# A rotary query turned by 32x32 blocks on VectorE, and stored in 128-byte runs, in an encoder layer on one core

## The chip, the core and the metric

One core of a Trainium2 chip runs the kernel. Its engines work side by side, each through its own list of instructions in order: TensorE (PE in the profile, its weight loads PEld), VectorE (DVE), ScalarE (ACT), GpSimd (POOL), and SyncE (SP), which here does nothing but issue DMAs. All DMAs of SP go through one queue: SP issues them one after the other, and one that waits for a semaphore holds up those behind it. The transfers themselves run on 16 DMA engines. The metric is the device time of one execution, in microseconds (us), the median of several.

## What is computed

One encoder layer on 2048 rows of 1024 columns, float32. A projection of the input feeds two groups of four heads. Group A is a gated linear attention in two directions, computed in chunks. Group B is a latent attention: queries and keys come from a compressed row by RMSNorm and a second matrix, and 64 of the query's 192 columns are rotary.

```python
q = (rms_norm(c_q, q_norm_g) @ w_uq).reshape(B, S, MLA_HEADS, MLA_D_NOPE + MLA_D_ROPE)
q_nope = q[..., :MLA_D_NOPE] * scale
q_rope = apply_rope(q[..., MLA_D_NOPE:], positions) * scale
...
s = (jnp.einsum('bqhd,bkhd->bhqk', qn, k_nope) + jnp.einsum('bqhr,bkr->bhqk', qr, k_r))
p = jax.nn.softmax(s, axis=-1)
return jnp.einsum('bhqk,bkhv->bqhv', p.astype(v.dtype), v)
```

Both groups' outputs go through one output projection, a residual and a LayerNorm. The change touches `q_rope`, 4 heads of 64 columns, on its way from the rows of a chunk (rows in the partitions) to the layout that the attention's matmuls need (the 64 rotary columns in the partitions, rows along the free dimension).

## The kernel before

Every float32 product is made of three matmuls: each operand is split into a high part (`hi`, line 353, on ACT by default) and a low part (`lo`, line 359, a subtraction on DVE, or on POOL where "pool" is given), and `mm3` (lines 407 to 409) multiplies high by high, high by low and low by high.

The work has four stages. The *first sweep* (to about 370 us) goes over the 16 chunks of 128 rows from the last to the first: group A's projections, the parts inside a chunk and the states of one direction, stored to DRAM. The *second sweep* (`sweep_c`, about 370 to 590 us) goes over the chunks forward, in eight steps of two chunks. The *attention* (about 590 to 1110 us) goes over 16 blocks (4 groups of 512 queries by 4 heads); for each it fetches the queries from DRAM. The *output projection* ends the kernel.

What the second sweep does for a chunk, by the names in the profile: `ipm` (line 1288) projects the chunk; `rm` is the RMSNorm's factor, `cq` and `ckv` (1311, 1315, ACT) the normed rows; `tm` (1341, PE) transposes them; `cqT`, `ckvT` and `krs` are their splits. `pqr` multiplies by the rotary columns, `qrf` (1478, DVE and, for the last add, 1376, POOL) applies the rotation, giving 128 rows by 4 heads by 64. Then, before the change:

- `c_tq` (1381): PE transposes two heads at a time, 128x128, into a PSUM tile `tq` of the pool `tr` (two buffers, shared with `tm` and `pqr`).
- `c_qrTh` and `c_qrTl`: ACT copies it as the high part and DVE subtracts for the low part, both of 128x256 from PSUM, into the tiles `qrTh` and `qrTl`, one buffer each for both chunks of a step.
- `c_sqr` (1265): four DMAs of SP per step, two for each part, each of 128 partitions by 1 KB, into the DRAM tiles `rh_s` and `rl_s` of the block group.

For group A, `Ob` (1435, PE) multiplies the query by the state, with the loads `qdb`, `SU`, `oib` and `ub` (1396, SP) from DRAM; `oib` is added on DVE (1438), then `og` (1458, DVE) norms and gates the result; a PSUM buffer of the pool `gp` comes free after it, which the next `Ob`, `pz` or `pq` needs. `oT` (1464) turns `og` by VectorE's 32x32 transposes, and `c_soT` (1470) stores it in four DMAs whose access patterns put the blocks in their places, in 128-byte runs, 64 KB each. Per step, `pz` (1217) projects the gate of group B from both chunks, `gm` is its SiLU, stored by `gm_s` (1238), and `pq` makes the other 128 query columns of each head, split into `qah` and `qal`, stored by `c_sqa` (1259).

**What sets the order.** Each function of the second sweep has a place: tables `PLACE_C`, `PLACE_C_FIRST` (step 0) and `PLACE_C_LAST` (step 7) give a pair of numbers for the two chunks, or one number for the step. `sweep_c` adds the step's number, sorts all by that sum and records them in this order with `in_order`, which makes each engine, SP too, keep it. So in SP's list the stores of step 5's rotary queries (5 + 1.869 = 6.869) stand right before the load of `oib` for chunk 14 (7 - 0.124 = 6.876), and those of step 6 (7.869) before chunk 14's `oa_s` (8.09). On ACT, chunk 14's `qrTh` (7 + 1.065) stands before chunk 15's `ckv` (7 + 1.075).

The attention has its own `in_order` list. Its first members on SP are the fetches of blocks 0 and 1 (lines 1520 and 1524: `qh`, `ql`, `rh`, `rl`, each `r` tile by two DMAs, one for each copy of the 64 rows, since the keys' high and low parts lie one under the other). They need buffers of the pool `wz`, which hold the weights of `pz` till the last `pz` of step 7. The two SP lists are merged when the kernel is built; neither is reordered in itself. Tiles with `bufs=1` are rewritten only when all that read them, DMAs too, have finished.

Of the kernel before, what the change touches and what calls it, by code (L numbers as in the profile page):

```python
# [9 lines left out]
F32 = mybir.dt.float32  # L10
F32R = mybir.dt.float32r
# [7 lines left out]
P = 128  # L19
# [4 lines left out]
H = 4  # L24
# [5 lines left out]
QB = 512  # L30
NQB = S // QB
# [113 lines left out]
    Ob=(0.141, 0.861),  # L145
    tm=(0.532, 1.152),
    pqr=(0.849, 1.355),
    tq=(1.06, 1.482),
    xh=(-0.19, -0.054),
    sqO=(0.272, 0.988),  # L150
    rgl=(0.283, 1.029),
# [6 lines left out]
    cqTh=(0.624, 1.184),  # L158
    ckvTh=(0.64, 1.277),
    krT=(0.848, 1.233),  # L160
    qrTh=(1.16, 1.587),
    oT=(0.392, 1.103),
    oib=(0.24, 0.881),
    ss=(0.278, 1.005),
# [5 lines left out]
    cqTl=(0.758, 1.284),  # L170
    ckvTl=(0.687, 1.321),
    qrf=(0.853, 1.411),
    qrTl=(1.25, 1.687),
    xl=(-0.154, 0.109),
    M=(-0.337, 0.299),
    Sf1=(-0.582, 0.202),
# [42 lines left out]
    Ob=(0.066, 0.896),  # L219
    tm=(0.445, 1.143),  # L220
    pqr=(0.716, 1.336),
    tq=(1.11, 1.512),
    xh=(-0.3, 1.403),
    sqO=(0.469, 0.999),
    rgl=(0.603, 1.027),
# [9 lines left out]
    qrTh=(1.276, 1.598),  # L235
# [11 lines left out]
    qrTl=(1.322, 1.703),  # L247
# [31 lines left out]
    Ob=(0.0, 0.299),  # L279
    tm=(0.495, 1.083),  # L280
    pqr=(0.749, 1.284),
    tq=(0.919, 2.161),
    xh=(-0.262, -0.109),
    sqO=(0.15, 0.374),
    rgl=(0.229, 0.457),
# [9 lines left out]
    qrTh=(1.065, 2.174),  # L295
# [11 lines left out]
    qrTl=(1.081, 2.186),  # L307
# [35 lines left out]
class K:  # L343
# [145 lines left out]
    def run(self):  # L489
        tc, nc, ins = self.tc, self.nc, self.ins  # L490
        with ExitStack() as top:
            cp = top.enter_context(tc.tile_pool(name="const", bufs=1))
            self.cp = cp
            dp = top.enter_context(tc.tile_pool(name="scr", bufs=1, space=DRAM))
            self.qd_s = [dp.tile([P, H * P], F32, name=f"qd_s{c}") for c in range(NCH)]
            self.oi_s = [dp.tile([P, H * P], F32, name=f"oi_s{c}") for c in range(NCH)]
            self.su_s = [dp.tile([P, H * P], F32, name=f"su_s{c}") for c in range(NCH)]
            self.u_s = [dp.tile([P, H * P], F32, name=f"u_s{c}") for c in range(NCH)]
            self.qa_s = [[dp.tile([P, H, QB], F32, name=f"q{p}_s{b}") for p in "hl"] for b in range(NQB)]
            self.qr_s = [[dp.tile([H, 64, QB], F32, name=f"r{p}_s{b}") for p in "hl"] for b in range(NQB)]  # L500
            self.gm_s = [dp.tile([P, H, QB], F32, name=f"gm_s{b}") for b in range(NQB)]
            self.oa_s = [dp.tile([P, H, P], F32, name=f"oa_s{c}") for c in range(NCH)]
            self.qk_s = [[dp.tile([64, H, P], F32, name=f"{n}_s{c}") for c in range(NCH)] for n in ("qx", "kx")]
            self.r_s = [dp.tile([1, H, QB], F32, name=f"r_s{b}") for b in range(NQB)]
            self.ob_s = [dp.tile([P, H, QB], F32, name=f"ob_s{b}") for b in range(NQB)]

            ident = cp.tile([P, P], F32, name="ident")
            self.ident = ident
            self.gkv_c = cp.tile([P, 1], F32, name="gkv_c")
            self.gn_c = cp.tile([P, 1], F32, name="gn_c")  # L510
            self.cw = cp.tile([P, NCH, 3, H], F32, name="cw")

            psum = ExitStack()
            pspool = lambda n: psum.enter_context(tc.tile_pool(name=n, bufs=2, space=PSUM, reuse_waits="tile"))
            self.gp, self.ip, self.tr = pspool("gp"), pspool("ip"), pspool("tr")
            self.xfp = top.enter_context(tc.tile_pool(name="xfp", bufs=2, reuse_waits="tile"))
            edge = top.enter_context(tc.tile_pool(name="edge", bufs=1, side="right"))
            edge.tile([P, 8], F32, name="edge")
            self.keep = top.enter_context(tc.tile_pool(name="keep", bufs=1, side="right", reuse_waits="tile"))
            wgs = ExitStack()  # L520
            self.wgp = wgs.enter_context(tc.tile_pool(name="wgp", bufs=2 * NK + 1, side="right", reuse_waits="tile"))
            self.xab = wgs.enter_context(tc.tile_pool(name="xab", bufs=2, side="right"))
            self.wgate = []
            self.wl = None
            self.sweep_a()
            self.wz = top.enter_context(tc.tile_pool(name="wz", bufs=2 * NK + 1, reuse_waits="tile"))
            bcs = ExitStack()
            self.wm = bcs.enter_context(tc.tile_pool(name="wm", bufs=2 * NK + 1, reuse_waits="tile"))
            self.bc = bcs.enter_context(tc.tile_pool(name="bc", bufs=1, reuse_waits="tile"))
            self.wl = bcs.enter_context(tc.tile_pool(name="wl", bufs=2, reuse_waits="tile"))  # L530
            self.late_gates()
            wgs.close()
            rp = top.enter_context(tc.tile_pool(name="res", bufs=1, side="right", reuse_waits="tile"))
            self.ckvT_h = rp.tile([P, NKT, P], F32R, name="ckvT_h")
            self.ckvT_l = rp.tile([P, NKT, P], F32R, name="ckvT_l")
            self.kr = rp.tile([P, NKT, P], F32R, name="krs")
            self.vh = rp.tile([P, NKT, P], F32R, name="vh")
            self.vl = rp.tile([P, NKT, P], F32R, name="vl")
            self.sweep_c()
            bcs.close()  # L540
            psum.close()
            self.wof = top.enter_context(tc.tile_pool(name="wof", bufs=PRE_W, side="right", reuse_waits="tile"))
            self.attention()
# [63 lines left out]
    def sweep_a(self):  # L607
        tc, nc, ins, cp = self.tc, self.nc, self.ins, self.cp
        with ExitStack() as ctx:
# [98 lines left out]
            step(0, {(1, 5): [("lrT", "cur")]})  # L708
            ch[1]["x"] = self.split_x(xp, xnext, NCH - 2, "xa", "dve", 2)
            run("bst", 0)  # L710
            self.wgr = [self.wgp.tile([P, 512], F32, tag="wg", name=f"wgr{k}") for k in range(NK)]
            for k, raw in enumerate(self.wgr):
# [12 lines left out]
            for i in range(4, NCH):  # L725
# [13 lines left out]
                if i == 12:  # L739
                    assert next(rope, None) is None  # L740
                    self.rope_tables(hpi)
            i = NCH - 1
            run("q", i)
            run("k", i)
            run("av", i - 1)
# [436 lines left out]
        self.wa[ct] = pa  # L1182

    def scale_w(self, ct):
        wa = self.w1.tile([P, H, P], F32, tag=f"qrT{'hl'[ct]}", name=f"wabs{ct}")
        self.nc.vector.scalar_tensor_tensor(wa, self.wa[ct], self.gq[:, ct:ct + 1],
                                            self.gkv_b[:, None, :].to_broadcast([P, H, P]), ALU.mult, ALU.mult)
        self.wa[ct] = wa
# [71 lines left out]

    def c_sqr(self, s):
        b, qs = self.of_step(s)
        for t, dst in zip(s["qrT"], self.qr_s[b]):
            for pr in range(2):
                self.nc.sync.dma_start(dst[2 * pr:2 * pr + 2, :, qs].rearrange("h d t -> (h d) t"),
                                       t[:, pr].rearrange("p a t -> p (a t)").bitcast(F32))


    def c_lx(self, d):
# [106 lines left out]
        self.nc.gpsimd.tensor_tensor(d["qr"], d["qr"], d["qrt"], ALU.add)  # L1376

    def c_tq(self, d):
        tq = d["tq"] = self.tr.tile([P, 4, P], F32, tag="tr", name=f"tq{d['c']}")
        for pr in range(2):  # L1380
            self.nc.tensor.transpose(tq[:, pr], d["qr"][:, 2 * pr:2 * pr + 2].rearrange("p h d -> p (h d)"), self.ident)

    def c_qrTh(self, d):
        s = d["step"]
        if "qrT" not in s:
            s["qrT"] = [self.w1.tile([P, 2, 2, P], F32R, tag=f"qrT{p}", name=f"qrT{p}{d['st']}") for p in "hl"]
        self.hi(s["qrT"][0][:, :, d["j"]], d["tq"][:, 0:2])

    def c_qrTl(self, d):
        qrT, j = d["step"]["qrT"], d["j"]  # L1390
        self.lo(qrT[1][:, :, j], d["tq"][:, 0:2], qrT[0][:, :, j])


    def gl_load(self, d, tag, src):
# [104 lines left out]
    def attention(self):  # L1499
        tc, nc = self.tc, self.nc  # L1500
# [3 lines left out]
        with ExitStack() as ctx:  # L1504
# [10 lines left out]
            def fetch(i):  # L1515
                h, b = blocks[i]
                q = stt[i]["q"] = []
                for p, src in zip("hl", self.qa_s[b]):
                    q.append(qp.tile([P, QB], F32R, tag="wz", name=f"q{p}{i}"))
                    nc.sync.dma_start(q[-1].bitcast(F32), src[:, h])  # L1520
                for p, src in zip("hl", self.qr_s[b]):
                    q.append(qp.tile([P, QB], F32R, tag="wz", name=f"r{p}{i}"))
                    for r in (slice(0, 64), slice(64, 128)):
                        nc.sync.dma_start(q[-1][r].bitcast(F32), src[h])

            def scores(i, j):

# [159 lines left out]
            def yc(i):  # L1687
# [3 lines left out]
                nc.sync.dma_start(self.ob_s[b][:, h], t)  # L1691

            fetch(0)
            fetch(1)
            wv = bp.tile([P, H * P], F32, tag="ofl", name="wvf", bufs=1)
            nc.sync.dma_start(wv, self.ins["wv"])
# [20 lines left out]
            for i in range(nb):  # L1717
                for j in range(NP):
                    t = NP * i + j
# [310 lines left out]
```

## Time and profile before

| | |
|---|---|
| time, 3 runs | 1277.12 us median (1277.0 to 1278.61) |
| the profiled execution | 1277.05 us; its span, first to last instruction, 1275.3 us |
| granted TensorE clock | 0.998 |
| busy in the span: PE, DVE, ACT, POOL | 1251.5, 898.4, 732.4, 720.1 us |
| PE busy from 0 to 370, 370 to 590, 590 to 1110 us | 360.88, 217.03, 517.12 us |
| DMA engines' mean share from 370 to 590 us | 0.67 |

How to read the profile's lines. A timeline row has the start in us, the duration in us, the engine, the line of the kernel, the operation, output and inputs by the program's names, shapes and the count of merged instructions; behind it in brackets stands the idle time of the engine before it and who ended it. SPq is SP's queue, and its duration is that of issuing the DMA, not of the transfer. A tile view gives for each line the count, then the shortest, median and longest duration in ns, and below "DMA to landing", from issue to arrival, in us. A row of the chain of waits has the start, how long the chain stays there, the engine, the tile and the line. A window row has the busy time of each engine in that stretch.

### The profile page before, as it was taken

Reading aid. Unit: us, or ns where it says so; the run is one execution under the profiler, and the core shown is the slowest. Engines: PE = TensorE matmul, PEld = TensorE weight load, DVE = VectorE, ACT = ScalarE, POOL = GpSimd, SP = SyncE. Lnnn points to the kernel's source line nnn. Section 1 sums busy time; section 2 is a strip of 40 time slices with the busy share of each in tenths; the row PEclk is TensorE's granted clock in tenths of the full one; section 3 lists DMA queues with packets and bytes.
Section 4 is the critical chain, followed back from the end, with each engine's and each line's share of the span. In section 5 each row is a group of like instructions: output and inputs, shape, how many; then the busy total and the mean of one; then the engine's idle time right before and its main releaser. Section 6 shows DMA issues by size and latency. Waiting matters only on the chain.

```text
span 1275.3 us, 19650 instructions
## 1 busy us (share of the span) xinstructions
PE 1251.5 (98%) x6986; PEld 1103.4 (87%) x6986; DVE 898.4 (70%) x1601; ACT 732.4 (57%) x1186; POOL 720.1 (56%) x443
## 2 busy tenths in 40 slices
PE   8999999999999999999999999999999999999997
PEld 7999999999899999989788888888888888887886
DVE  6635454544565555554888888888888888479997
ACT  7544444454565544544888888788888888511110
POOL 0132323232345555520598888889999999935541
PEclk9999999999999999999999999999999999999999
DMA  8223434334757777657201111111233110376652
GB/s 292 79 81 110 114 110 115 109 100 114 244 199 205 221 208 206 186 153 219 76 9 49 42 52 52 44 31 58 58 92 91 42 43 10 124 235 195 211 192 99
DMA packets 167233, 155.24 MB, mean 122 GB/s; under 512 B 77046, under 2 KB 119678, under 8 KB 167136
## 3 DMA queue, kind: packets, MB, share of 16 engines
q1 hardware_dynamic: 159072, 151.86, 40.0%
q0 software_dynamic: 672, 2.10, 0.4%
q8 instruction: 55, 0.90, 0.3%
q10 hardware_dynamic: 7392, 0.03, 0.3%
q14 instruction: 42, 0.34, 0.1%
HBM read 100.43 MB, written 53.51 MB: 121 GB/s over the span
## 4 chain that ended last, share of the span: by engine, by line
PE 84%; DVE 5%; DMA 4%; ACT 2%; issue 2%; SPq 2%; POOL 0%; DVEq 0%; ACTq 0%; POOLq 0%
PE pz L1217 7%; PE ipm L1288 5%; PE o L407 4%; PE o L408 4%; PE o L409 4%; PE pS L1534 4%; PE pS L1536 4%; PE pS L1537 4%; PE pS L1538 4%; PE pS L1535 4%; PE ipa L407 4%; PE ipa L409 4%; PE ipa L408 4%; PE ipg L407 2%; PE ipg L408 2%; PE ipg L409 2%
## 5 line engine op out<-in xcount | busy, mean ns | idle before, releaser
L359 POOL TENSOR_TENSOR pl<-s,ph 128x1024 fp32r<-128x1024 f32 x128 | 306.6, 2414 | 53.0 <-ACT ph L353 49.2
L1556 DVE TENSOR_TENSOR rm<-pS,rm 128x512 f32<-128x512 f32 x210 | 144.9, 690 | 35.7 <-ACT s L1543 30.4
L1543 ACT ACTIVATE s<-pS 128x1024 f32<-128x1024 f32 x128 | 131.2, 1025 | 60.6 <-PE pS L1538 51.4
L1580 DVE TENSOR_TENSOR s<-s,mb 128x1024 f32<-128x1024 f32 x128 | 151.2, 1214 | 9.5 <-PE mb L1574 8.8
L353 ACT ACTIVATE ph<-s 128x1024 fp32r<-128x1024 f32 x128 | 135.0, 1056 | 17.2 <-PE o L409 16.5
L1584 ACT ACTIVATE s<-s 128x1024 f32<-128x1024 f32 x128 | 131.3, 1049 | 11.0 <-DVE s L1580 10.9
L407 PE MATMUL ipa<-wah,xah 128*128 128x384 f32 (+1 forms) x384 | 130.1, 339 | 5.1 <-ACT wah L353 5.1
L408 PE MATMUL ipa<-wal,xah 128*128 128x384 f32 (+1 forms) x384 | 124.9, 325 | 0.0
L409 PE MATMUL ipa<-wah,xal 128*128 128x384 f32 (+1 forms) x384 | 124.7, 325 | 0.0
L1534 PE MATMUL pS<-qh,ckvT_h 128*128 128x512 f32 x256 | 102.5, 400 | 0.8 <-DVE rm L1556 0.4
L407 PE MATMUL o<-ph,vh 128*128 128x512 f32 x256 | 101.0, 395 | 0.0
L409 PE MATMUL o<-ph,vl 128*128 128x512 f32 x256 | 99.8, 390 | 0.0
L1537 PE MATMUL pS<-rh,krs 128*128 128x512 f32 x256 | 99.8, 390 | 0.0
L1536 PE MATMUL pS<-qh,ckvT_l 128*128 128x512 f32 x256 | 99.8, 390 | 0.0
L1538 PE MATMUL pS<-rl,krs 128*128 128x512 f32 x256 | 99.7, 389 | 0.0
L1535 PE MATMUL pS<-ql,ckvT_h 128*128 128x512 f32 x256 | 99.7, 389 | 0.0
L408 PE MATMUL o<-pl,vh 128*128 128x512 f32 x256 | 99.7, 389 | 0.0
L1054 POOL TENSOR_TENSOR Sb<-Sb,Us 64x512 f32<-64x512 f32 x15 | 20.9, 1394 | 137.0 <-DVE Us L1046 127.9
L1607 DVE TENSOR_TENSOR ap<-ap,s 128x512 f32<-128x512 f32 x120 | 83.1, 693 | 2.6 <-ACT s L1584 0.7
L407 PEld LDWEIGHTS ipa<-wah,xah 128*128 128x128 f32 x384 | 73.2, 191 | 7.8 <-ACT wah L353 5.5
L359 POOL TENSOR_TENSOR ol<-of,oh 128x512 fp32r<-128x512 f32 x32 | 43.4, 1357 | 64.0 <-ACT oh L353 63.3
L359 POOL TENSOR_TENSOR xal<-xaf,xah 128x1024 fp32r<-128x1024 f32 x12 | 29.7, 2477 | 87.8 <-ACT xah L353 87.8
(301 smaller groups left out, 3485.8 us busy)
## 6 DMA issues: line engine op xcount, KB each, us to landing
xcf<-xT_dram SPq DMA_DIRECT2D x16, 512.0 KB, 5.3
xr<-x_dram SPq DMA_DIRECT2D x16, 512.0 KB, 6.7
out_dram<-rr SPq DMA_DIRECT2D x32, 256.0 KB, 2.1
xaf<-xT_dram SPq DMA_DIRECT2D x14, 512.0 KB, 3.9
oib<-oi_s SPq DMA_DIRECT2D x16, 256.0 KB, 3.7
qdb<-qd_s SPq DMA_DIRECT2D x16, 256.0 KB, 3.4
SU<-su_s SPq DMA_DIRECT2D x16, 256.0 KB, 4.0
ub<-u_s SPq DMA_DIRECT2D x16, 256.0 KB, 3.9
```

What stands on the lines that cost most here:

```text
L353: return nc.scalar.activation(dst, src, AF.Copy).ins
L359: return e.tensor_tensor(dst, src, hi.bitcast(F32), ALU.subtract).ins
L407: mm(out, ah, bh, start=start, stop=False)
L408: mm(out, ah, bl, start=False, stop=False)
L409: mm(out, al, bh, start=False, stop=stop)
L1534: mm(ps[:, e], kh, qh, start=True, stop=False)
L1535: mm(ps[:, e], kh, ql, start=False, stop=False)
L1536: mm(ps[:, e], kl, qh, start=False, stop=False)
L1537: mm(ps[:, e], kr, rh, start=False, stop=False)
L1538: mm(ps[:, e], kr, rl, start=False, stop=True)
L1556: V.tensor_tensor(d["rm"], src[:, e], d["rm"], ALU.max)
L1580: V.tensor_tensor(s, s, d["mb"][:, None, :].to_broadcast([P, 2, QB]), ALU.subtract)
```

## The change

The PE transposes of the rotary queries go. `c_tq` now turns the 128x256 tile by VectorE's transposes of 32x32 blocks, from SBUF to a new SBUF tile `qrx` (one buffer). `hi` and `lo` read that tile instead of PSUM; they write one tile `qrT` that holds both parts of both chunks of a step, in one buffer. Since a block transpose leaves the blocks where they were, the store puts them in place: `c_sqr` makes eight DMAs per step, each of 32 partitions by 16 runs of 128 bytes, 64 KB, into one DRAM tile per block group, `qr_s`, with the rows of a 32-row block outermost. The fetch of a block reads each `r` tile by four DMAs of 32 partitions by 2 KB instead of two of 64. The places of `tq`, `qrTh` and `qrTl` move back a little: `tq` from (1.06, 1.482) to (1.13, 1.56), `qrTh` from (1.16, 1.587) to (1.19, 1.62), `qrTl` from (1.25, 1.687) to (1.26, 1.7), and `tq` of the first step to (1.15, 1.53), of the last to (0.95, 2.1). The buffer of `qrT` also serves a setup tile, `wabs`, as the two old ones did.

```diff
-            self.qr_s = [[dp.tile([H, 64, QB], F32, name=f"r{p}_s{b}") for p in "hl"] for b in range(NQB)]
+            self.qr_s = [dp.tile([32, 2, H, 2, QB], F32, name=f"qr_s{b}") for b in range(NQB)]
...
     def c_sqr(self, s):
         b, qs = self.of_step(s)
-        for t, dst in zip(s["qrT"], self.qr_s[b]):
-            for pr in range(2):
-                self.nc.sync.dma_start(dst[2 * pr:2 * pr + 2, :, qs].rearrange("h d t -> (h d) t"),
-                                       t[:, pr].rearrange("p a t -> p (a t)").bitcast(F32))
+        dst = self.qr_s[b].rearrange("r p h a (c e t) -> e r (p h a) c t", c=4, e=4)
+        for j in range(2):
+            t = s["qrT"][:, j].rearrange("p a (m t) -> p (a m) t", t=32).bitcast(F32)
+            for e in range(4):
+                self.nc.sync.dma_start(dst[e, :, :, qs.start // P + j], t[32 * e:32 * e + 32])
...
     def c_tq(self, d):
-        tq = d["tq"] = self.tr.tile([P, 4, P], F32, tag="tr", name=f"tq{d['c']}")
-        for pr in range(2):
-            self.nc.tensor.transpose(tq[:, pr], d["qr"][:, 2 * pr:2 * pr + 2].rearrange("p h d -> p (h d)"), self.ident)
+        d["tq"] = self.w1.tile([P, 256], F32, tag="qrx", name=f"qrx{d['c']}")
+        self.nc.vector.transpose(d["tq"], d["qr"].rearrange("p h d -> p (h d)"))

     def c_qrTh(self, d):
         s = d["step"]
         if "qrT" not in s:
-            s["qrT"] = [self.w1.tile([P, 2, 2, P], F32R, tag=f"qrT{p}", name=f"qrT{p}{d['st']}") for p in "hl"]
-        self.hi(s["qrT"][0][:, :, d["j"]], d["tq"][:, 0:2])
+            s["qrT"] = self.w1.tile([P, 2, 2, 256], F32R, tag="qrT", name=f"qrT{d['st']}")
+        self.hi(s["qrT"][:, d["j"], 0], d["tq"])

     def c_qrTl(self, d):
         qrT, j = d["step"]["qrT"], d["j"]
-        self.lo(qrT[1][:, :, j], d["tq"][:, 0:2], qrT[0][:, :, j])
+        self.lo(qrT[:, j, 1], d["tq"], qrT[:, j, 0])
...
-                for p, src in zip("hl", self.qr_s[b]):
+                for n, p in enumerate("hl"):
                     q.append(qp.tile([P, QB], F32R, tag="wz", name=f"r{p}{i}"))
-                    for r in (slice(0, 64), slice(64, 128)):
-                        nc.sync.dma_start(q[-1][r].bitcast(F32), src[h])
+                    for r in range(4):
+                        nc.sync.dma_start(q[-1][32 * r:32 * r + 32].bitcast(F32), self.qr_s[b][:, n, h, r % 2])
```

More of the change, by code (lines that the diff above doesn't have):

```diff
@@ L160 @@
     krT=(0.848, 1.233),
-    qrTh=(1.16, 1.587),
+    qrTh=(1.19, 1.62),
     oT=(0.392, 1.103),
@@ L172 @@
     qrf=(0.853, 1.411),
-    qrTl=(1.25, 1.687),
+    qrTl=(1.26, 1.7),
     xl=(-0.154, 0.109),
@@ L221 @@
     pqr=(0.716, 1.336),
-    tq=(1.11, 1.512),
+    tq=(1.15, 1.53),
     xh=(-0.3, 1.403),
```

8 lines of the change are left out of this document (5 added, 3 removed).

## The prediction

> **What bounds the kernel now.** The page first: TensorE (PE) is busy nearly all the time. Then the busy times by stretch, in the second sweep (370 to 590 us) and at its end; the columns are the stretch, its length, the busy us of PE, PEld, DVE, ACT and POOL with their instructions, the clock, the DMA engines' share and GB/s.
>
> ```profile
> span 1275.3 us, 19650 instructions
> PE 1251.5 (98%) x6986; PEld 1103.4 (87%) x6986; DVE 898.4 (70%) x1601; ACT 732.4 (57%) x1186; POOL 720.1 (56%) x443
> ...
> 385.00:545.00 160.00, 160.00 (x1185) 156.13 (x1185) 88.40 (x320) 77.88 (x226) 85.00 (x91) 1.00 0.72 206
> 545.00:575.00 30.00, 27.03 (x171) 24.40 (x170) 18.58 (x67) 14.94 (x41) 9.25 (x11) 1.00 0.51 142
> 470.00:472.00 2.00, 2.00 (x13) 1.82 (x13) 1.79 (x11) 1.06 (x4) 2.00 (x2) 1.00 0.80 120
> ```
>
> From 385 to 545 us PE never rests, and VectorE (DVE) works 88.4 of 160 us. In the next 30 us PE loses 3.0 us. So an instruction taken from PE is worth its place in PE's row up to 545 us; after that one must read what PE waits for. The timeline of SyncE's queue (SP), the chain of waits, the view of the tile oib and the timelines of DVE and PE show that seam:
>
> ```profile
> 553.50 0.85 SPq L1265 DMA_DIRECT2D rh_s<-qrTh  x2
> 554.45 0.96 SPq L1265 DMA_DIRECT2D rl_s<-qrTl  x2
> 555.46 1.05 SPq L1396 DMA_DIRECT2D oib<-oi_s  x2
> 556.55 2.71 SPq L1470 DMA_DIRECT2D oa_s<-oT  x4
> 559.30 0.81 SPq L1238 DMA_DIRECT2D gm_s<-gm  x1
> ...
> 555.46 4.19 DMA oib<-oi_s
> ...
> DMA to landing us min/median/max: 2.8/3.7/7.7
> ...
> 559.74 0.70 DVE L1438 TENSOR_TENSOR Ob<-Ob,oib 128x512 f32<-128x512 f32 x1 [3.72 <-DMA oib<-oi_s]
> ...
> 562.30 0.94 PE L1435 MATMUL Ob<-SU,qdb 128*128 128x128 f32 x6 [2.07 <-DVE og L1458]
> ...
> 572.95 0.39 PE L1217 MATMUL pz<-xch,wzh 128*128 128x256 f32 x1 [0.20 <-DVE og L1458]
> ```
>
> SP issues in order. Step 5's four rotary stores (L1265) stand right ahead of the load of oib for chunk 14; DVE waits 3.72 us for that load, and PE 2.07 us for DVE. From there to 572.95 DVE hardly pauses, and PE starts step 7's pz when DVE lets it. Whatever lengthens those four stores lengthens the kernel.
>
> **The change, part by part.** *PE loses 32 transposes.*
>
> ```profile
> L1381 PE MATMUL tq<-ident,qrf x32: 270/272/283, 386.0 to 589.5; 128*128 128x128 f32 x32
> ...
> 386.19 0.22 PE tq L1381 x2
> ...
> 539.73 0.22 PE tq L1381 x2
> ```
>
> Each lasts 272 ns, but matmuls overlap; in the chain a pair takes 0.22 us. Chunks 0 to 11 have theirs between these two rows: 12 x 0.22 = 2.6 us off PE before 545 us. Sixteen pairs would make 3.5.
>
> *DVE gains 16 transposes of 128x256, SP gains stores.* The output of the linear attention already goes this way, with 128x512 transposes and stores of 64 KB in 128-byte runs:
>
> ```profile
> L1470 SPq DMA_DIRECT2D oa_s<-oT x64: 573/631/1042, 384.1 to 593.7; - x64
> L1464 DVE STREAM_TRANSPOSE oT<-og x16: 711/712/715, 376.7 to 572.9; 128x512 f32<-128x512 f32 x16
> ...
> DMA to landing us min/median/max: 2.2/3.3/5.9
> ...
> L359 DVE TENSOR_TENSOR qrTl<-tq,qrTh x16: 409/415/426, 390.6 to 590.9; 128x256 fp32r<-128x256 f32 x16
> ```
>
> A 128x256 transpose lies between half of 712 ns and all of it. DVE's add of 512 columns above took 0.70 us and its subtraction of 256 took 0.415, so 256 columns are 0.28, and I take 0.712 - 0.28 = 0.43 us. In the steady part DVE has 45% idle, and this is hidden. Its new wait is for POOL's qrf add; behind it on DVE stand og and qal, but that add is on POOL already, some us ahead of the split in every steady step, so I count nothing (uncovered, each chunk would cost up to 0.43). ScalarE and DVE now read the turned tile from SBUF instead of PSUM, at the same 256 columns: nothing either way, at most the 0.02 us that the split's own rows scatter.
>
> Each step's rotary stores become eight of 512 runs of 128 bytes instead of four of 1 KB runs. The row to go by is oa_s, equal in size and runs: four of them hold SP from 556.55 to 559.30, 2.75 us, so eight take 5.5 (bounds 5.0, from the 573 ns minimum and 0.05 between, and 6.2). The four old ones took 553.50 to 555.46, 1.96. SP gains **3.5 us** per step. In a steady step this is covered:
>
> ```profile
> 459.01 0.87 SPq L1265 DMA_DIRECT2D rh_s<-qrTh  x2
> 459.97 0.90 SPq L1265 DMA_DIRECT2D rl_s<-qrTl  x2
> 466.99 0.32 SPq L1396 DMA_DIRECT2D qdb<-qd_s  x1
> ...
> 472.63 0.38 ACT L353 ACTIVATE qrTh<-tq 128x256 fp32r<-128x256 f32 x1
> ```
>
> After the stores SP idles 6.1 us until a PE matmul frees qdb. Their last one would be issued at 463.8 and land at 467.1, and the one buffer qrT is rewritten only at 472.63. The new layout's transfers cost DMA time: the window from 470 to 472, nearly all oa_s stores, moved 120 GB/s at a share of 0.80, against 206 at 0.72 on average, so 512 KB need 3.4 us of all 16 DMA engines instead of 1.8, 0.06 more share in a 28.5 us step. They don't fill.
>
> *At the seam it isn't covered.* All before it comes 2.6 us earlier. Then eight stores stand ahead of oib: +3.5. The load itself took 4.19 us behind a full queue; behind small stores I take 3.7, the median of all oib loads (bounds 2.8, their minimum, and 4.19): -0.5. PE's wait at 562.30 ends at -2.6 + 3.5 - 0.5 = +0.4. Chunk 12's transpose falls into DVE's chain: pz starts at +0.83.
>
> ```profile
> 573.56 1.19 DVE L359 TENSOR_TENSOR qal<-pq,qah 128x1024 fp32r<-128x1024 f32 x1
> ...
> 575.42 2.08 SPq L1265 DMA_DIRECT2D rh_s<-qrTh  x2
> ...
> 581.29 0.56 SPq L1520 DMA_DIRECT2D ql<-ql_s  x1
> ...
> 583.17 1.19 SPq L1524 DMA_DIRECT2D rl<-rl_s  x2
> ...
> 581.36 0.38 ACT L353 ACTIVATE qrTh<-tq 128x256 fp32r<-128x256 f32 x1 [0.84 <-PE tq L1381]
> 581.64 0.36 ACT L1315 ACTIVATE ckv<-ipm,rm_r 128x128 f32<-128x128 f32 x1
> ...
> 582.59 0.38 PE L1341 MATMUL tm<-ident,cq 128*128 128x128 f32 x2
> 590.54 0.39 PE L1538 MATMUL pS<-rl,krs 128*128 128x512 f32 x1
> ```
>
> Chunk 13's transpose now precedes qal on DVE, so step 6's stores start at 575.42 + 0.83 + 0.43 = 576.7; the eighth is issued 7 x 0.69 later, at 581.5, and lands after 3.3 (bounds 2.2 and 5.9) at 584.8. Only then may ScalarE (ACT) write chunk 14's qrTh into the one qrT buffer. Behind it stands ckv of chunk 15, which PE's tm needs: 584.8 + 0.28 + 0.36 = 585.5, where tm ran at 582.59. PE alone would be there at 582.59 + 0.83 - 0.22 = 583.2. **tm comes 2.9 us late**; chunk 15's pair gives back 0.22, so the attention starts at +2.7.
>
> *The fetch.* Each block of queries now takes eight pieces instead of four, at some 0.6 us (the two at 583.17 take 1.19). For block 0: stores end 582.2, oa_s 2.75 later at 584.9, ql at 585.6, last piece issued at 589.8. With the 3.3 us of a 64 KB store it lands at 593.1; PE wants it at 590.54 + 2.7 = 593.2. With the 4.19 of the oib load it costs 0.8, so I count 0.3. In later blocks SP has idle time, and PE, busy without a break, passes the shift on to the end.
>
> Sum: -2.6 + 3.5 - 0.5 + 0.43 + 2.1 (the rest of the late tm) - 0.22 + 0.3 = **+3.0 us**. The profiled execution took 1277.05, 1.75 more than its span and 0.07 under the median 1277.12; 1277.05 + 3.0 = 1280.05, say **1280.1**. With all low bounds (stores 5.0, load 2.8, landing 2.2) the seam passes at -1.0 and tm isn't late: 1276.7. With all high ones (6.2, 4.19, landing 4.4) tm comes 5.8 late: 1283.
>
> The Trainium skill, DMA: Bandwidth & Descriptors, section "Specifications", wants runs of at least 512 B, since smaller ones are read, modified and written; by that the stores should land later than those of 1 KB. The trace shows 3.3 us for 64 KB in 128-byte runs, so the sum stays.
>
> **Rivals.** (1) *PE's saving stands; faster.* Here the bytes ahead of a load delay it, not the issues: the same 512 KB stand ahead of oib and of qrT's release as before, both come as early as now, and all 16 pairs count: 1277.05 - 3.5 = 1273.6. It decides if eight stores take SP no longer than about 2 us. Against it: eight at the 573 ns minimum make 4.6. The Trainium skill, same page, section "Issuing engines are not separate DMA queues", calls the sequencer's time to initiate a DMA usually small relative to the DMA itself, which is this rival; the trace disagrees, at 631 ns of issue each.
>
> (2) *Only the oib load is late, the buffer is free in time* (stores land in 2.2 us): -2.6 + 3.5 - 0.5 + 0.43 - 0.4 (two pairs) = +0.4: 1277.5.
>
> (3) *The fetch of block 0 falls behind step 7's stores.*
>
> ```profile
> 585.55 0.45 SPq L1524 DMA_DIRECT2D rh<-rh_s  x1
> 590.60 0.58 SPq L1238 DMA_DIRECT2D gm_s<-gm  x1
> 591.24 3.10 SPq L1470 DMA_DIRECT2D oa_s<-oT  x4
> 594.43 1.04 SPq L1265 DMA_DIRECT2D rh_s<-qrTh  x2
> ...
> 596.51 0.57 SPq L1259 DMA_DIRECT2D qh_s<-qah  x1
> ...
> 597.81 1.05 SPq L1524 DMA_DIRECT2D rh<-rh_s  x1
> ```
>
> The sweep's own SP order is fixed and so is the attention's, but the two are merged when the kernel is built. The merge cut block 1's rh in two: one piece at 585.55, the other behind gm_s, oa_s, the stores and qa of step 7, although SP idles 4.6 us on the chip. From 575.42 to gm_s there are 4 + 4 + 8 issues. If the merge again grants 16, the stores take 8, oa_s 4, and only ql and three pieces go ahead; the other five follow step 7's stores. Then gm_s starts at 593.3, and 0.64 + 3.19 + 5.5 + 1.30 bring 603.9; the fifth piece is issued at 606.3 and lands at 609.6, 16.4 after PE wants it: 1277.05 + 2.7 + 16.4 = 1296.2. For it: the cut is there. Against: a merge by bytes would leave it where it is.
>
> **Chances.** Forecast 0.48 (its own range 1276.7 to 1283), rival 1 0.12, rival 2 0.08, rival 3 0.32. The range reaches from 1276 to 1297.5: it leaves out rival 1 and the top of rival 3, 0.18 together. This kernel's measurement tells about 0.2% (2.6 us) from no change. Faster by more than that: 0.11, most of rival 1. Within: 0.26, rival 2 and the lower third of the forecast. Slower: 0.63.
>
> **What would show it.** In the changed profile: no tq on PE, and PE about 2.6 us ahead at 545; eight rotary stores over about 5.5 us ahead of oib, and DVE's wait for oib; ACT's qrTh of chunk 14 released by stores, with tm behind it; where block 0's pieces stand against step 7's gm_s. I am wrong if the stores issue quicker than oa_s, if loads and stores stand in another order on SP, or if DVE's wait for POOL shows in the steady part.

## The result, and the profile after

The changed kernel takes 1296.99 us (median of 4 runs, 1296.84 to 1297.34), the kernel before 1277.86 us beside it on the same chip (4 runs, 1277.0 to 1278.7): a ratio of 1.0148, 95% interval 1.0133 to 1.0163. It is 19 us slower. The profiled execution took 1297.34 us at a granted clock of 0.991. In the code of the kernel after, the lines of before stand 2 to 4 further down.

The page's head, and of its costliest groups the last product of the scores, with the idle time ahead of it in the last column:

```profile
span 1295.6 us, 19721 instructions
...
PE 1251.1 (97%) x6954; PEld 1103.3 (85%) x6954; DVE 905.1 (70%) x1617; ACT 733.8 (57%) x1186; POOL 721.1 (56%) x443
...
L1540 PE MATMUL pS<-rl,krs 128*128 128x512 f32 x256 | 100.4, 392 | 15.1 <-DMA rl<-qr_s 15.1
```

PE has 32 instructions fewer and nearly the same busy time; one single wait of 15.1 us is most of the loss. The timeline of SP's queue through the seam shows where it comes from:

```profile
550.94 6.59 SPq L1269 DMA_DIRECT2D qr_s<-qrT  x8
557.57 1.10 SPq L1398 DMA_DIRECT2D oib<-oi_s  x2
...
578.14 6.21 SPq L1269 DMA_DIRECT2D qr_s<-qrT  x8
...
587.13 0.56 SPq L1522 DMA_DIRECT2D ql<-ql_s  x1
587.79 1.77 SPq L1526 DMA_DIRECT2D rh<-qr_s  x4
589.66 0.83 SPq L1526 DMA_DIRECT2D rl<-qr_s  x2
594.59 0.57 SPq L1240 DMA_DIRECT2D gm_s<-gm  x1
595.21 3.10 SPq L1472 DMA_DIRECT2D oa_s<-oT  x4
598.41 5.50 SPq L1269 DMA_DIRECT2D qr_s<-qrT  x8
...
605.31 2.25 SPq L1526 DMA_DIRECT2D rl<-qr_s  x2
```

Block 0's `rl` is cut in the middle. Two of its four pieces go at 589.66; then SP idles 4 us until step 7's gate is ready, issues that step's gate, output, rotary and content stores, and only at 605.31 the other two pieces. Nothing on the chip asks for this: the pieces were in their place in the attention's list, and the list was merged so when the kernel was built. PE's timeline (in brackets the idle time before the row) and, below it, the clock by stretch (stretch, length, PE busy, clock, DMA share, GB/s):

```profile
563.81 2.08 PE L1437 MATMUL Ob<-SU,qdb 128*128 128x128 f32 x8 [6.35 <-DVE og L1460]
575.37 0.39 PE L1219 MATMUL pz<-xch,wzh 128*128 128x256 f32 x1 [0.42 <-DVE og L1460]
586.73 0.33 PE L1344 MATMUL tm<-ident,ckv 128*128 128x128 f32 x1 [1.54 <-ACT ckv L1318]
593.39 0.39 PE L1536 MATMUL pS<-qh,ckvT_h 128*128 128x512 f32 x1
609.63 0.77 PE L1540 MATMUL pS<-rl,krs 128*128 128x512 f32 x1 [15.14 <-DMA rl<-qr_s]
```

```profile
561.00:566.00 5.00, 2.19 (x9) 0.61 0.93 227
566.00:575.00 9.00, 8.95 (x52) 0.84 0.37 85
...
609.00:611.00 2.00, 1.37 (x3) 0.50 0.79 210
611.00:613.00 2.00, 2.00 (x6) 0.50 0.82 229
```

PE's rows against before's make a ledger of the loss. The last `pz` ahead of the seam gives way to `ipm` at 543.43 (before 545.96): 2.5 us ahead. The `Ob` that waits starts 1.5 us late (563.81, before 562.30), the next `pz` 2.4 late (575.37, before 572.95), `tm` behind `ckv` some 4 late (586.73, before 582.59 for the whole group), the scores 3.9 late (593.39, before 589.54), and the first L1540 19.1 late (609.63, before 590.54). Then the clock is at half for another 3.6 us: a product of the scores takes 0.43 us there and 0.23 later. The first `mx` starts at 631.45 (before 611.49), 20.0 late, and the span ends 20.3 late. Behind the first scores hardly anything more is lost.

### The profile page after: what moved, and what is told of

It is laid out like the page before. It is cut to its first block, busy times and chain, and to the rows that moved or that the text cites. A ratio compares the mean times of both kernels' runs of the same rounds, so it can differ in the third digit from the quotient of the medians.

```text
span 1295.6 us, 19721 instructions
## 1 busy us (share of the span) xinstructions
PE 1251.1 (97%) x6954; PEld 1103.3 (85%) x6954; DVE 905.1 (70%) x1617; ACT 733.8 (57%) x1186; POOL 721.1 (56%) x443
## 4 chain that ended last, share of the span: by engine, by line
PE 83%; DVE 5%; DMA 4%; ACT 3%; SPq 2%; issue 2%; POOL 0%; DVEq 0%; ACTq 0%; POOLq 0%
PE pz L1219 6%; PE ipm L1291 5%; PE o L407 4%; PE o L408 4%; PE o L409 4%; PE pS L1540 4%; PE pS L1536 4%; PE pS L1537 4%; PE pS L1538 4%; PE pS L1539 4%; PE ipa L407 4%; PE ipa L409 4%; PE ipa L408 4%; PE ipg L407 2%; PE ipg L408 2%; PE ipg L409 2%
## 5 line engine op out<-in xcount | busy, mean ns | idle before, releaser
L1540 PE MATMUL pS<-rl,krs 128*128 128x512 f32 x256 | 100.4, 392 | 15.1 <-DMA rl<-qr_s 15.1
```

The costliest lines, as they stand in the source:

```text
L1540: mm(ps[:, e], kr, rl, start=False, stop=True)
```

## The experiments

The theory after the result: PE's saving is real (2.5 us by the seam), the seam takes it back with some 6 us because SP's queue is held by the stores, and 15 us come from the cut that the merge of SP's two lists makes in block 0's fetch. The rival: short runs or VectorE's transposes themselves do the harm, in whatever order. All times are medians; each chip ran the kernel before as well, so the ratios compare, not the microseconds of different chips. "First mx" is the start of that PE instruction in the profile.

| kernel | us | before, same chip | ratio (95%) | first mx, us |
|---|---|---|---|---|
| before | 1277.86 | | | 611.5 |
| after | 1296.99 | 1277.86 | 1.0148 (1.0133 to 1.0163) | 631.5 |
| first_fetch | 1281.19 | 1277.32 | 1.0028 (1.0018 to 1.0038) | 615.6 |
| old_runs | 1273.65 | 1277.32 | 0.9968 (0.9958 to 0.9978) | 608.7 |
| before_runs | 1277.43 | 1277.32 | 1.0002 (0.9989 to 1.0015) | 612.8 |
| before_small | 1293.42 | 1277.32 | 1.0124 (1.0105 to 1.0143) | 629.4 |
| late_store | 1280.36 | 1278.42 | 1.0013 (1.0004 to 1.0023) | 612.7 |
| two_qrT | 1280.30 | 1278.42 | 1.0014 (1.0004 to 1.0023) | 614.1 |
| halves | 1283.27 | 1278.42 | 1.0040 (1.0026 to 1.0055) | 615.5 |
| halves_late | 1282.75 | 1278.42 | 1.0035 (1.0024 to 1.0046) | 614.8 |
| late_two | 1274.13 | 1277.22 | 0.9977 (0.9967 to 0.9986) | 609.2 |
| four_fetch | 1277.28 | 1277.22 | 1.0004 (0.9994 to 1.0013) | 612.1 |
| four_best | 1273.86 | 1277.22 | 0.9972 (0.9963 to 0.9982) | 607.8 |
| before_late | 1274.95 | 1277.31 | 0.9985 (0.9976 to 0.9994) | 609.2 |

### first_fetch: the same transfers, the fetch whole

```diff
+    def fetch_q(self, i):        # the ten loads of a block, as fetch had them
...
+            self.early = {}
+            todo.append((8.5, len(todo), self.early_q, (0,)))
...
             def fetch(i):
-                ...
+                stt[i]["q"] = self.early.pop(i) if i in self.early else self.fetch_q(i)
```

> The changed kernel with one thing moved: block 0's ten loads of rotary and content queries are recorded in the sweep's own list, between the output stores of chunk 14 and step 7's gate store, so that SP gets all of them ahead of step 7's eight rotary stores. Same transfers, same run lengths. Theory (SP's order of issue cuts block 0's fetch in two): PE's wait of 15.1 us at L1540 goes to under 1, and with it some 2 us of matmuls at half clock; what is left is the seam of steps 5 and 6, so 1279.7 (1278 to 1282). Rival (runs of 128 bytes crowd the DMA engines, so that the pieces land late in whatever order they are issued): PE still waits over 5 us there, 1286 or more.

It took 1281.19 us: from 1.0148 to 1.0028 of the kernel before. PE's longest waits in this kernel's seam (us in total, times, longest):

```profile
PE Ob L1454 <- DVE og L1477: 6.0, 1, 6.0
PE tm L1361 <- ACT ckv L1335: 1.5, 1, 1.5
...
PE pS L1549 <- DMA rl<-qr_s: 0.7, 2, 0.4
```

The 15.1 us are gone, with no transfer changed. So the cut in SP's order cost 1.2% of the time, some 15 us, the half clock behind it included. The seam's two waits stay.

### before_small and before_runs: PE's transposes back, only the stores changed

before_small splits the four stores by 32 partitions, in runs of 1 KB; before_runs splits them into eight of 512 runs of 128 bytes.

```diff
 # before_small
-            for pr in range(2):
-                self.nc.sync.dma_start(dst[2 * pr:2 * pr + 2, :, qs]..., t[:, pr]...)
+            for e in range(4):
+                self.nc.sync.dma_start(to[32 * e:32 * e + 32], frm[32 * e:32 * e + 32])
 # before_runs
+            for pr in range(2):
+                to = dst[2 * pr:2 * pr + 2, :, qs].rearrange("h d (m e t) -> e (h d) m t", e=2, t=32)
+                frm = t[:, pr].rearrange("p a (m e t) -> e p (a m) t", e=2, t=32).bitcast(F32)
+                for e in range(2):
+                    self.nc.sync.dma_start(to[e], frm[e])
```

> The kernel before with PE's transposes and eight stores a step of 64 KB, still in runs of 1 KB (64 runs in each): the number of SP's issues as in the changed kernel, the length of the runs as before. In SP's list block 0's fetch is now cut: three pieces stand behind step 7's gate, output, rotary and content stores. Theory (number of issues and the cut in SP's list): PE waits 8 to 15 us at the first scores, 1286 to 1295; if SP issues these stores faster than 0.63 us each, the seam's share is smaller. Rival (the run length is the cost): within 1 us of the kernel before, 1277 to 1279.

It took 1293.42 us, 1.0124 of before. The waits and SP's timeline of before_small:

```profile
PE pS L1538 <- DMA rh<-rh_s: 13.9, 1, 13.9
PE Ob L1436 <- DVE og L1459: 2.4, 1, 2.4
```

```profile
584.57 0.49 SPq L1525 DMA_DIRECT2D rh<-rh_s  x1
591.88 0.56 SPq L1238 DMA_DIRECT2D gm_s<-gm  x1
592.49 3.09 SPq L1471 DMA_DIRECT2D oa_s<-oT  x4
...
597.78 2.08 SPq L1267 DMA_DIRECT2D rl_s<-qrTl  x4
...
601.20 1.04 SPq L1525 DMA_DIRECT2D rh<-rh_s  x1
```

No transpose on VectorE and no short run, and nearly the same loss, from the same kind of cut in SP's order. Here four more issues a step were enough to move the cut; this is the plainest evidence for the theory's main part.

> The kernel before with PE's transposes, and only its stores changed: eight stores a step of 64 KB, each 512 runs of 128 bytes, as in the changed kernel; the fetch stays in two pieces for each tile and SP's list has block 0's fetch whole ahead of step 7's stores. Theory (each such store costs SP 0.63 us; the seam suffers, the fetch does not): the wait at Ob grows from 2.07 to some 6, the wait of tm behind ckv appears, no wait of PE over 1 us at the first scores; 1277.9 + 4 to 6.5 = 1282 to 1284.4. Rival (runs of 128 bytes by themselves make block 0's fetch late): 1290 or more.

Here both sides missed: 1277.43 us, no difference from before. The fetch is whole, as the theory said; step 7's gate store follows only at 592.40:

```profile
585.77 1.13 SPq L1526 DMA_DIRECT2D rh<-rh_s  x2
586.99 1.19 SPq L1526 DMA_DIRECT2D rl<-rl_s  x2
```

Yet this kernel has the same eight issues a step as before_small, where the fetch is cut. So the number of issues alone does not decide where the merge cuts.

The wait at `Ob` grew (3.7 us, from 2.1), but by 1.6 us and not by 4, and `tm` has no wait. Two reasons can be read from the profiles. First, its stores are cheaper for SP. The tile views give the issue's duration in ns (shortest, median, longest), for before, after, before_small and before_runs in turn:

```profile
L1265 SPq DMA_DIRECT2D rh_s<-qrTh x16: 382/428/1578, 400.7 to 595.0; - x16
```

```profile
L1269 SPq DMA_DIRECT2D qr_s<-qrT x64: 550/627/1860, 400.6 to 603.3; - x64
```

```profile
L1267 SPq DMA_DIRECT2D rh_s<-qrTh x32: 382/427/1125, 401.2 to 597.2; - x32
```

```profile
L1268 SPq DMA_DIRECT2D rh_s<-qrTh x32: 360/561/1136, 400.9 to 598.1; - x32
```

By the medians an issue costs 0.43 us whether it holds 128 KB or 64 KB in runs of 1 KB. With 512 runs of 128 bytes it costs 0.56 from 128 partitions (0.51 for the low part's stores) and 0.63 from 32. At the seam this made 4.5 us for eight, where the changed kernel needed 6.6. Second, before_runs keeps two tiles, `qrTh` and `qrTl`; the high part's four stores go first, so the tile that ACT writes next is free four stores earlier. The changed kernel holds both parts in one tile, free only when the last of the eight has landed. The second reason is argued, not shown alone.

### old_runs: the transposes on VectorE, the stores and the fetch of before

```diff
-        dst = self.qr_s[b].rearrange("r p h a (c e t) -> e r (p h a) c t", c=4, e=4)
-        for j in range(2): ...
+        for p, dst in enumerate(self.qr_s[b]):
+            for j in range(2):
+                self.nc.sync.dma_start(dst[2 * j:2 * j + 2, :, qs]..., s["qrT"][:, j, p].bitcast(F32))
```

> VectorE's transposes kept, the stores and the fetch as in the kernel before: four stores of 128 KB in runs of 1 KB for each step, block fetches in two pieces for each rotary tile. The rotary queries so stored stand in a wrong arrangement, which leaves the scores' values and not their work changed. Theory (the loss is all in the stores and what they push back on SP): the seam returns to the kernel before's, and PE's saving stands: pz ends 2.5 us earlier, 1274.4 (1273 to 1276). Rival (VectorE's transposes cost what PE saves, through og at the seam): 1277 or more.

It took 1273.65 us, 0.9968 of before, a little under the forecast 1274.4 and inside its range. So the work that the change moves from PE to VectorE is worth 3.7 us by the medians (2.8 to 5.4 by the interval), which agrees with the prediction's first term, 2.6 to 3.5 us, and VectorE's transposes cost nothing that shows. All of the loss is in the stores, the fetch and what stands behind them on SP.

### late_store and two_qrT: the two waits of the seam, one at a time

```diff
 # late_store, on first_fetch (in put)
+                p = 2.05 if (n, st) == ("sqr", len(steps) - 3) else p
 # two_qrT, on first_fetch
-            s["qrT"] = self.w1.tile([P, 2, 2, 256], F32R, tag="qrT", name=f"qrT{d['st']}")
+            s["qrT"] = self.w1.tile([P, 2, 2, 256], F32R, tag="qrT", name=f"qrT{d['st']}", bufs=2)
```

> The changed kernel with block 0's fetch whole ahead of step 7's stores (as in first_fetch, 1281.2 us), and step 5's eight rotary stores moved behind chunk 14's and 15's oib loads in the sweep's list. Theory (PE's wait at Ob comes from the oib load that stands 6.3 us behind these stores on SP): oib is issued some 6 us earlier, the wait at Ob falls from 6.0 to under 1, PE keeps its full clock there; part comes back, since the one buffer of qrT is then let go later, near 561.5, for the chunk after: 1276 (1274 to 1278). Rival (og is late through VectorE's own transposes, or through ub): the wait stays over 4 us, 1280 or more.

The wait at `Ob` went as the theory said (0.69 us), and the time hardly did: 1.0013 against first_fetch's 1.0028, well over the 1276 that was expected. PE's and VectorE's timelines of late_store show why:

```profile
557.66 1.16 PE L1455 MATMUL Ob<-SU,qdb 128*128 128x128 f32 x8 [0.69 <-DVE og L1478]
562.07 0.39 PE L409 MATMUL pqr<-wqr_h,cqT_l 128*128 128x256 f32 x1 [1.81 <-DVE cqT_l L359]
...
566.83 0.58 PE L407 MATMUL pq<-cqT_h,wabs_h 128*128 128x256 f32 x1 [1.51 <-DVE og L1478]
583.73 0.33 PE L1362 MATMUL tm<-ident,ckv 128*128 128x128 f32 x1 [0.78 <-ACT ckv L1336]
```

```profile
560.80 0.43 DVE L359 TENSOR_TENSOR qrT<-qrx,qrT 128x256 fp32r<-128x256 f32 x1 [0.25 <-ACT qrT L353]
...
565.65 1.12 DVE L1478 SCALAR_TENSOR_TENSOR og<-Ob,rg_r,ub 128x128 f32<-128x128 f32 x4 [2.78 <-DMA ub<-u_s]
```

The stores moved past oib now stand ahead of chunk 14's `ub`, for which VectorE waits 2.78 us, and they let the one buffer go late. PE's clock falls to a half from about 564 us, too (last section). One queue, and still 6.8 us of issues: whatever stands behind them is late.

> first_fetch (1281.2 us) with a second buffer for the transposed rotary queries, nothing else. Theory (the wait of 1.5 us of tm behind ckv comes from step 6's stores, which hold the one buffer until they have landed): that wait goes, the wait of 6.0 at Ob stays: 1279.7 (1278.7 to 1280.6). Rival (ScalarE is late for another reason, or the time is lost again right behind, at pz or the gates): 1281 or more.

It took 1280.30 us; the wait of `tm` is gone and the 6.1 us at `Ob` stay, as the theory said. From 1.0028 to 1.0014 the intervals overlap, so the gain itself is only likely (first `mx` 1.5 us earlier).

### halves and halves_late: half of the stores early

```diff
 # halves, on first_fetch: "sqr0" ahead of "sqr", four stores each
+    sqr0=1.33,
     sqr=1.869,
...
+    def c_sqr0(self, s):
+        self.c_sqr(s, 0)
 # halves_late adds late_store's line
```

> first_fetch (1281.2 us) with each step's eight rotary stores in two groups of four: those of the step's first chunk go as soon as that chunk is split, while SP has nothing to do, those of the second where all eight stood. The last step is left as it was. Theory: only four stores (3.2 us) stand ahead of chunk 14's oib, so the wait at Ob goes from 6.0 to about 2.8, and with the buffer free 3 us earlier the wait of tm goes too: 1276 (1274.5 to 1277.5). Rival (the stores do their harm as traffic on the DMA engines and not by SP's order): no gain, 1280 or more.

> halves, with the second group of step 5's stores behind the two oib loads as in late_store. Theory: no store stands ahead of oib and the buffer of qrT is free in time; both waits of the seam go (Ob under 1 us, tm none), and the 2.5 us that PE saved before the seam stand: 1273.5 (1271.5 to 1275), faster than both kernels. Rival: PE's saving is used up at the seam by another wait (pz or the gates behind og): 1276 or more.

Both missed: 1.0040 and 1.0035, no faster than first_fetch. These times lie in the rivals' ranges, but at the seam the theory held: the wait at `Ob` is 2.0 us in halves and gone in halves_late, with the same bytes on the DMA engines, and `tm` has no wait there. The loss lies in the steady steps this time: PE had 62.1 and 62.9 us of work between 385 and 450 us, where it had 65.0 in the kernel before and in first_fetch. SP's timeline of halves:

```profile
385.96 0.89 SPq L1420 DMA_DIRECT2D oib<-oi_s  x1
390.65 2.57 SPq L1276 DMA_DIRECT2D qr_s<-qrT  x4
...
413.73 0.31 SPq L1420 DMA_DIRECT2D SU<-su_s  x1
419.96 2.58 SPq L1276 DMA_DIRECT2D qr_s<-qrT  x4
422.58 0.62 SPq L1420 DMA_DIRECT2D oib<-oi_s  x1
```

The early stores were put where their data isn't ready: SP waits 3.8 and 5.9 us for them, and the loads behind them, which were ready to go, wait too. The stores were early in the list and not early on the chip; a bad place, so these two say nothing on half stores well placed.

### late_two: both waits at once

late_store's line with 2.3 in place of 2.05 (behind `ub` too), and two_qrT's second buffer.

> first_fetch (1281.2 us) with a second buffer for the transposed rotary queries, and step 5's eight stores on SP behind chunk 14's and 15's oib loads, step 6's first output store, its gate store and chunk 14's ub load. Theory (the seam's loss is what stands on SP behind these stores, first oib, then ub, and the one buffer; late_store moved the wait from oib to ub and to the buffer): no wait of PE over 1 us from 545 us to the first scores, full clock there, first mx near 608 us where the kernel before has 611.5: 1273.5 (1271.5 to 1276). Rival (PE's saving is always eaten by a next wait, as it was in late_store): a new wait of 2 us or more in the seam, 1278 or more.

It took 1274.13 us, 0.9977 (0.9967 to 0.9986) of before: the theory's number within 0.7 us, and faster than both kernels. Its PE timeline has no wait over 1.2 us in the seam, and the clock stays at 1.00:

```profile
558.23 1.16 PE L1455 MATMUL Ob<-SU,qdb 128*128 128x128 f32 x8 [0.37 <-DVE og L1478]
561.95 0.39 PE L409 MATMUL pqr<-wqr_h,cqT_l 128*128 128x256 f32 x1 [1.11 <-DVE cqT_l L359]
```

### four_fetch and four_best: half as many stores

```diff
-            self.qr_s = [dp.tile([32, 2, H, 2, QB], F32, name=f"qr_s{b}") for b in range(NQB)]
+            self.qr_s = [dp.tile([32, 4, 2, H, 2, P], F32, name=f"qr_s{b}") for b in range(NQB)]
...
-        for j in range(2):
-            t = s["qrT"][:, j].rearrange("p a (m t) -> p (a m) t", t=32).bitcast(F32)
-            for e in range(4):
-                self.nc.sync.dma_start(dst[e, :, :, qs.start // P + j], t[32 * e:32 * e + 32])
+        t = s["qrT"].rearrange("p j a (m t) -> p (j a m) t", t=32).bitcast(F32)
+        for e in range(4):
+            self.nc.sync.dma_start(dst[e].rearrange("r c m t -> r (c m) t"), t[32 * e:32 * e + 32])
```

> first_fetch (1281.2 us) with four rotary stores a step of 128 KB, each 1024 runs of 128 bytes, in place of eight of 512 runs: both chunks of a step go in one transfer; the scratch is laid out by 128 tokens, so each piece of a fetch reads runs of 512 bytes. Theory A (an issue has a base price on SP, 0.43 us as with 64 runs of 1 KB, and 512 runs of 128 bytes add 0.2): 0.83 us each, 3.3 us a step, half of what eight take; the wait at Ob falls from 6.0 to about 3, that of tm goes: 1277.5 (1276 to 1279). Theory B (SP's price goes by the number of runs): 1.25 us each, 5 us a step, little changes: 1280 to 1281.5.

The time, 1277.28 us, is in theory A's range, but the sum is neither theory's. SP's queue and PE's timeline of four_fetch:

```profile
550.54 4.47 SPq L1271 DMA_DIRECT2D qr_s<-qrT  x4
555.05 1.12 SPq L1416 DMA_DIRECT2D oib<-oi_s  x2
```

```profile
561.08 2.08 PE L1455 MATMUL Ob<-SU,qdb 128*128 128x128 f32 x8 [4.23 <-DVE og L1478]
...
583.36 0.33 PE L1362 MATMUL tm<-ident,ckv 128*128 128x128 f32 x1 [1.42 <-ACT ckv L1336]
```

At the seam an issue took 1.1 us on average, nearer to B's 1.25 than to A's 0.83; the wait at `Ob` fell to 4.2, not to 3, and that of `tm` stayed. Half as many issues with twice the runs save about 30% of the queue's time (first_fetch's eight took 6.34 us there).

> late_two with the four stores a step of four_fetch. Theory: no store stands ahead of a load that PE waits for, so what is left to win is small: 1273 (1271 to 1275.5). Rival (transfers of 1024 short runs hold up the DMA queue that the loads share): behind late_two by 2 us or more.

It took 1273.86 us, 0.9972 (0.9963 to 0.9982), level with late_two, as the theory said. Of the kernels that store the queries in the arrangement the attention needs it has the lowest time, though not measurably ahead of late_two.

### before_late: what the order is worth without the change

late_two's two edits on the kernel before, with PE's transposes and its four stores.

> The kernel before, PE's transposes and its four stores of 1 KB runs kept, with late_two's two other edits: step 5's rotary stores behind chunk 14's oib and ub loads, and a second buffer for the transposed rotary queries. Theory (late_two's 3.1 us under the kernel before are both: PE's transposes gone, 2.5 us, and part of the seam's wait of 2.07): these edits alone bring at most that wait: 1275.6 (1274.8 to 1276.8). Rival 1 (the whole gain of late_two is that of the list on SP): 1274.3 or less. Rival 2 (the list brings nothing with four stores, the transposes all): within 0.3 us of the kernel before.

It took 1274.95 us, 0.9985 (0.9976 to 0.9994): the two edits alone bring 2.4 us by the medians, about the wait of 2.07 us at `Ob`, which is gone from its profile. So of late_two's 0.23% two thirds are theirs by the medians. Its interval overlaps this one, and so does four_best's: what VectorE's transposes add once the list is right was too small to be told apart here. With the stores and the fetch of before they are worth 0.32% (old_runs), in before's own order.

The profiles of late_two and before_late show where PE's saving goes. late_two is ahead when the scores start, 586.06 us against 587.28. Then its PE waits 1.4 us for block 0's pieces (0.57 for `ql`, 0.28 for `rh`, 0.51 for `rl`), for which before_late's PE does not wait, and the first `mx` starts at 609.20 in the one and 609.23 in the other. No run tried another place for that fetch.

## Why the prediction was right or wrong

The forecast was 1280.1 us, with 0.48 of the chance, and the kernel takes 1296.99; what happened is rival 3, given 0.32 and 1296.2. The step of the forecast that failed is **the fetch**, counted at 0.3 us on the assumption that all of block 0's pieces go ahead of step 7's stores. Two pieces did not, and first_fetch and before_small show that this order alone made the difference. The sign of the change was right. That the range held is owed to rival 3 alone, for which it reached up to 1297.5; the forecast's own range ended at 1283. With the fetch kept whole the change costs 3.9 us (first_fetch), so the rest of the forecast's +3.0 was right within a microsecond.

Point by point:

- *PE's saving*, -2.6 us by 545: 2.5 in the trace. old_runs shows that it lasts to the end when nothing takes it back.
- *VectorE's transposes*, 0.43 us, hidden in the steady part: the tile view of `qrx` has a median of 436 ns, and PE worked without a pause from 385 to 543 us. The price and the hiding were right, the wait for POOL counted at nothing was not:

```profile
L1383 DVE STREAM_TRANSPOSE qrx<-qrf x16: 402/436/445, 385.9 to 594.5; 128x256 f32<-128x256 f32 x16
...
  POOL qrf L1379: 6.4, 7
```

  VectorE's wait for POOL does show, 6.4 us in seven waits, six of them (5.4 us) in the steady part. The prediction had named that as a sign of being wrong; but none of it reaches PE, so it cost nothing.
- *The eight stores at 5.5 us*: a size that was off. They took 6.59 and 6.21 us at the seam, and 5.50 to 7.04 us in the eight steps. The median price of one (627 ns) was that of the row used (631), but some issues in each group are slower (one of 1.66 us in the 6.59), and the two groups of the seam came to 0.82 and 0.78 us each. The wait at `Ob` ended at +1.5 instead of +0.4: 1.1 us of it are these.
- *The DMA engines' share*, 0.06 more: 0.78 instead of 0.72 from 385 to 545 us. Right, and it goes with the short runs: 0.77 in before_runs, 0.72 in before_small. PE did not wait for it.
- *oib's load*, 3.7 us: 3.58 from issue to landing. Right.
- *pz at +0.83*: +2.4. 1.1 of the difference is the late end of the wait at `Ob`. The rest, 0.5, are two gaps of VectorE ahead of that `pz`, 0.22 us before `qrT` at 566.91 and 0.29 before `og` at 574.19, where before has none; why VectorE paused there is open.
- *tm 2.9 late by way of the one buffer*: the mechanism was right (ACT's `qrT` of chunk 14 waits 1.70 us for the stores, `ckv` stands behind it, `tm` waits 1.54 for that; two_qrT takes this wait away). `tm` was some 4 late, since step 6's stores began at 578.14 and not at 576.7, and landed 2.2 us after the last issue rather than 3.3.
- *The fetch's issues at 0.6 us each*: 0.44 for the four of `rh` (1.77 us), cheaper than counted. first_fetch has all eight pieces and ten loads issued by 592.8, and PE waits at most 0.4 us for any: without the cut the step would have been right within a microsecond.
- *Rival 3* had the mechanism, and its argument against itself, a merge that counts bytes, is refuted by before_small, whose bytes are those of before. Its count was off, seven loads ahead and two pieces behind instead of four and five; that hardly moved the price, because the wait is set by step 7's stores: 15.1 us measured, 16.4 predicted. It missed the half clock behind the wait, with which PE took 21.8 us from the first product with `rl` to the first `mx`, where before took 20.95.
- *Rival 1's condition*, eight stores in no longer than about 2 us, failed in the changed kernel itself (6.59 us). That bytes and not issues delay a load is refuted by before_runs, where the same bytes in eight issues lengthen the wait at `Ob` by 1.6 us. The size of PE's saving in it was real, as old_runs shows.

The rule by which the merge cuts has not been found. It is not a count of 16 issues, as rival 3 supposed: from step 6's first rotary store to step 7's gate store SP makes 16 in before, 14 in before_small, 17 in before_runs and 19 in the changed kernel. It was only shown that four more issues a step can move the cut into block 0 (before_small) and need not (before_runs), and that recording the fetch in the sweep's list removes it. Rival 3 with 0.32 against 0.48 was too low in one respect: the quoted row of before already showed the merge cutting a fetch with 16 issues between, and the change adds issues exactly there.

## What to carry to other kernels

On a queue that issues in order, count issues and their price, not bytes: when a step's stores double in number, list every load behind them until the next idle time, and expect that moving the stores past one load hands the wait to the next (late_store), until the stores stand behind all of them and their buffer is doubled (late_two). Where two ordered lists are merged at build time, read the merged order of the changed kernel before anything else: here one cut cost 15 us and the engine work that the change is about 2.5. And when a tidied version is faster, give the tidying to the old kernel too; here that alone brought 0.15%, and what the change adds to it could not be measured.

## What the runs showed of the hardware

- PE's granted clock fell to a half after short idle times. An idle of 2.07 us (before) cost no clock. After one of 2.45 us (before_small) the eight products of `Ob` took 1.54 us instead of 1.16, and the granted clock was 0.52 from 564 to 567 us; after one of 2.79 us (old_runs) the eight took 2.08 us, and the same after 4.23 and 6.35 us; after 15.14 us the products of the scores ran at 0.43 us each for 3.6 us. By windows of half a us, the half clock lasted 3.4 us in old_runs and before_small, and 6.8 us at the seam of the changed kernel, of first_fetch and of late_store. The Trainium skill, TensorE: Matmul & The Clock Gate, section "Why this matters for your kernels", asks for no gap of PE over about 3 us. Here 2.45 us was already too much, and the longest gap alone did not decide: in late_store no gap is over 1.81 us, and yet the clock fell. Its mean of 0.84 from 560 to 566 us means a half clock from about 564 us on, behind gaps of 1.81 and 0.58 us and ahead of the third, of 1.51:

```profile
560.00:566.00 6.00, 2.93 (x13) 1.71 (x11) 2.43 (x12) 1.76 (x8) 3.46 (x4) 0.84 0.82 189
566.00:570.00 4.00, 3.17 (x15) 3.17 (x16) 3.60 (x11) 0.86 (x3) 0.73 (x1) 0.50 0.46 98
```

- The price of an issue on SP went by the shape of the transfer: a median of 0.43 us in runs of 1 KB, for 64 KB and 128 KB alike, and 0.51 to 0.56 and 0.63 us for 512 runs of 128 bytes from 128 and from 32 partitions. The median is not the price of a group, since single issues take much longer: in four_fetch the median for 1024 runs is 0.63 us, too, but four of them took 3.89 to 5.71 us, 1.1 each on average.
